# Memory-attention heads with a longer distance from scores to transposes, S5 phases by angle doubling, u tiles in the key buffers, and the last output tile in halves

## The chip, the cores and the metric

The kernel runs on one core of one Trainium2 chip. The metric is the device time of one execution in microseconds; a time quoted as "of the runs" is the median of several executions, and the profile is one further execution recorded by the hardware profiler. The engines are TensorE (PE, its weight loads PEld), VectorE (DVE), ScalarE (ACT), GpSimd (POOL) and SyncE (SP, which here only issues DMAs).

## What is computed

One layer of an encoder block, for a prompt of 256 tokens and a sample of 512 tokens together (768 rows, width 1024), all in 32-bit floats:

```python
h = rmsnorm(x, norm_mix_g)
u, q, k, v, qm, gl = split(h @ w_in)
# A) S5: bidirectional complex-diagonal scan over u (64 groups of 16 channels, 64 states each)
lam_bar = exp(lam * dt);  b_bar = ((lam_bar - 1) / lam) * b
s[t] = lam_bar * s[t-1] + b_bar @ u[t];   y = Re(c @ s)  (forward + backward) + d * u
z = gelu(y); s5_out = z * sigmoid(z @ s5_w_glu)
# B) differential attention, 8 heads, two softmax maps per head
# C) cross-attention of qm into 256 memory tokens, 4 heads of 256 channels:
kv = rmsnorm(mem) @ w_kv; q, k = rmsnorm per head
p = softmax(q @ k.T / 16); mem_out = p @ v
x = x + (sum over branches of sigmoid(gl + b_gate) * (branch @ w_branch)) @ w_out
x = x + (silu(h2 @ w_gate) * (h2 @ w_up)) @ w_down        # h2 = rmsnorm(x)
```

The outputs are the two blocks of rows of x.

## The kernel before

Every large product is done with each operand split into a high and a low part (suffixes `h` and `l`), as three matmuls of 128 x 128 weights against 256 or 512 columns (`mm3`, lines 831 to 833). `split_evac` (823, 824) makes the two parts of a PSUM result: ACT copies the high part, DVE subtracts. Weights arrive through `WStream`: SP loads a raw tile `wr` (567), ACT makes `wh` (666), DVE makes `wl` (672).

The program is written as one long Python function, `hybrid_block`. Dense projections are the base load of PE; the smaller stages are generators that are advanced between dense units by a `Pace` object: each dense unit calls `tick(w)`, and the generator makes `rate * w` steps. The written order is not the final one. A planner of the compiler takes the written order as priority, simulates the engines with its own costs, and fixes one order for each engine at compile time; on the chip each engine then works through its own queue strictly in that order, waiting on semaphores. A tile is given a buffer by name (`tag`) with a number of buffers (`bufs`); a new tile of a tag waits until the tile that held its buffer is done with, and a pool that takes over the memory of a closed pool waits for what lay there.

The stages around the change, with their places in the profiled execution:

- **Memory keys, values and queries** (from the start to about 212 us): `MEM_ORDER` k0 k1 v0 v1 k2 q0 q1 v2 k3 q2 v3 q3. The raw keys of a head lie in `kr` (three buffers in the pool `ma1`, right side of SBUF). `mem_q` writes the head's queries into `mqh`/`mql`, one buffer each, so the queries of head h+1 can be written only after the last scores of head h.
- **Memory attention**, `mem_attend`, paced through these units from q1 on and on through the first u chunks: for each head it sums squares (`qss`, 1008), makes the reciprocal root `rq`, and then takes the six tiles of 128 rows. Step i does the scores of tile i (`ms`, six matmuls into one of two PSUM banks of pool `a`; DVE takes the maximum, 1037; ACT the exponential, 1042; DVE normalizes `mp`, 1044), and the two transposes of tile i-1 (`mpT`, 1054). After two tiles ACT and DVE move the transposed weights into `pTh`/`pTl`, and in steps 3 and 7 PE multiplies them with the values (`mo`), which go to HBM (`mo_scr`, SP, 1027).
- **S5 parameters**, `S5.params` and `S5.pack`: short DVE instructions on 128 x 64 numbers, paced through the same units; ACT adds two sines of half the angle (`sn`, `cs`) and two of eight times the angle (`th8`, results `xr` and `p8r`, lines 138 and 140). `pack` scales matrices into `par` tiles (ACT copies, 263 and 264; DVE, 230) and stores them (`p_scr`).
- **u chunks**, `u_chunk` (from 215 us): the S5 input u is computed in four chunks of two tiles `ut`. POOL clears three columns of a new tile (293), DVE and ACT copy the PSUM results in (1183, 1181), and SP flushes the tile to HBM (`u_scr`, 298). Chunks 0 and 1 take their tiles from a pool `utp` of two buffers on the left side of SBUF; chunks 2 and 3 from `utp2` on the right side, where `ma1` was.
- **S5 steps**, `S5.steps` (from about 273 us): 16 groups, in 57 pieces, paced through u chunks 2 and 3 and the 12 gate chunks `gl`. `fetch` loads `par` on SP (280, 281) into the pool `s5q` on the left side; `build` makes `G` on DVE (308 to 317); `response` multiplies `G` (`psK`, 343).
- **Differential attention**, `diff_attend`, paced through the q/k/v units and, at `DIFF_TAIL` steps a unit, through the first branch product `br` (877 to 984 us); its scores are `sc` (1380, 1381), its transposes `aT`, its value products `av` (1417).
- **The last products**, `down_last`: two halves of the rows, each with two column blocks of three tiles of 128 x 512; `into` adds each PSUM bank to `x` (1626) and SP stores it (1628).

Of the kernel before, what the change touches and what calls it, by code (L numbers as in the profile page):

```python
# [24 lines left out]
class S5:  # L25
# [32 lines left out]
    def params(self, scratch):  # L58
# [85 lines left out]
        yield from exp_parts(ldt, dt)  # L144
        xr = tt(t("xr"), lre, dt, mul)
        th = tt(t("th"), lim, dt, mul)
        er, em1 = t("er"), t("em1")
        yield from exp_parts(xr, er, em1)
        thr = reduce_2pi(th, th)
        yield  # L150
        sn, cs = sincos(tsc(t(), thr, 0.5, None, mul), t("sn"), t("cs"))
        th8 = reduce_2pi(t("th8"), tsc(t(), thr, 8.0, None, mul))
        tsc(self.v8, th8, 1.0 / TWO_PI, None, mul)
        yield
        p8i, p8r = sincos(th8, xr, t("p8r"))
        s2 = tt(t(), sn, sn, mul)
        cm1 = tsc(t("cm1"), s2, -2.0, None, mul)
        sinth = stt(t(), sn, 2.0, cs, mul, mul)
        Lr = stt(t("Lr"), cm1, 1.0, er, add, mul)
        Li = tt(t("Li"), er, sinth, mul)  # L160
        yield

# [35 lines left out]
        pwi = scratch.tile([128, 8, 64], F32, name="pwi")  # L198
        tmp = scratch.tile([128, 4, 64], F32, name="pwt")
        nc.gpsimd.memset(pwr[:, 0, :], 1.0)  # L200
# [87 lines left out]

    def u_tile(self, pool, mt):

        ut = pool.tile([128, 8, NK], F32, name=f"ut{mt}", tag="ut")
        for c in (0, 33, 98):
            self.nc.gpsimd.memset(ut[:, :, c : c + 1], 0.0)
        return ut
# [212 lines left out]
TILES = 6  # L507
S5_RATE = 0.68
PAR_RATE = 0.7
PACK_RATE = 0.8  # L510
MEM_RATE = 1.45
DIFF_TAIL = 1.8
DIFF_RATE = 6.0 / 9.0
# [184 lines left out]
def hybrid_block(ctx, tc, A, outs, consts):  # L698
# [20 lines left out]
    def uid(s):  # L719
        cnt[0] += 1  # L720
        return f"{s}_{cnt[0]}"
# [275 lines left out]
    def mem_attend():  # L997

        for h in range(4):
# [13 lines left out]
            P, PT = {}, {}  # L1013
            for i in range(TILES + 2):
                if i in (3, 7):
                    sg = 0 if i == 3 else 1
                    c0, n = SEGS[sg]
                    for e in range(2):
                        mo = [k2.tile([128, 512], F32R, name=uid("mo" + w), tag="mo" + w) for w in "hl"]
                        ps = env.psb("mo")  # L1020
                        es = slice(128 * e, 128 * e + 128)
                        for c in range(2):
                            mm3(ps[:, 0:n], vv[0][:, 2 * sg + c, es], vv[1][:, 2 * sg + c, es],
                                PT[0][:, c, 0:n], PT[1][:, c, 0:n], c == 0, c == 1)
                        split_evac(mo[0][:, 0:n], mo[1][:, 0:n], ps[:, 0:n])
                        for w in range(2):
                            nc.sync.dma_start(mo_scr[w][:, 2 * h + e, c0 : c0 + n], mo[w][:, 0:n].bitcast(F32))
                if i < TILES:
# [10 lines left out]
                    v.tensor_tensor(out=nm, in0=nm, in1=r_, op=mul)  # L1039
                    p = k2.tile([128, 256], F32, name=uid("mp"), tag="mp", bufs=2)  # L1040
                    s = sm.tile([128, 1], F32, name=uid("mss"), tag="mss")
# [3 lines left out]
                    P[tt] = p  # L1045
                if 1 <= i <= TILES:
                    tt = i - 1
                    sg = 0 if tt < 2 else 1
# [4 lines left out]
                    for c in range(2):  # L1053
                        pe.transpose(pT[:, 256 * c + 128 * t : 256 * c + 128 * t + 128],
                                     p[:, 128 * c : 128 * c + 128], env.ident)
                    if tt in (0, 2):
                        PT = tuple(P3["k3"].tile([128, 2, 512], F32R, name=uid("pT" + w), tag="pT" + w) for w in "hl")
# [128 lines left out]

    mat.rate = 1.5
    def both(w):
# [8 lines left out]
    qctx.close()  # L1197
    uctx = ExitStack()
    up = uctx.enter_context(tc.tile_pool(name="utp2", bufs=2, side="right"))

    with ExitStack() as c2:
# [3 lines left out]
        pace = Pace(s5.steps(y_scr), S5_RATE)  # L1205
        u_chunk(2, pace.tick)
        u_chunk(3, pace.tick)
# [414 lines left out]

    def into(r, c, y, done=False):
        for t in range(3):
            o = out_block(r, c, t)
            v.tensor_tensor(out=o, in0=o, in1=y[t], op=add)
# [6 lines left out]
    def rows_times(ps, left_, right_, start, stop):  # L1633
# [46 lines left out]
    def down_last(fb):  # L1680
# [3 lines left out]
        for r in range(2):  # L1684
            h = slice(HT * r, HT * r + HT)
            x = [L.pop("A11") if r == 0 else left("A21", a[:, :, h]), left("A2", b[:, :, h])]
            if r == 0:
                down_sums(1)
                down_sums(2)
            ps = [banks(), banks()]  # L1690
            for i in range(2):
                for c in range(2):
                    y = [(lambda k, j=j: w[i](k, 512 * c, 512)[j]) for j in range(2)]
                    rows_times(ps[c], x[i], y, i == 0, i == 1)
            for c in range(2):
                into(r, c, ps[c], done=True)

# [453 lines left out]
```

## Time and profile before

| | |
|---|---|
| median of 3 runs | 1741.17 us (1739.56 to 1742.98) |
| the profiled execution | 1741.41 us |
| its span, first to last instruction | 1739.3 us |
| PE busy | 1713.9 us (99%), 11312 matmuls |
| DVE busy | 1340.6 us (77%) |
| ACT busy | 935.9 us (54%) |
| mean granted TensorE clock | 0.996 |

The execution's time is 2.1 us more than its span. A busy PE in these pages means that some matmul was in flight, not that it ran at its peak. A view of waits lists who sat idle until whom; a view of windows gives busy time and the granted clock (1.00 is full speed) in a stretch; the chain is the work that ended last, followed back.

### The profile page before, as it was taken

Reading aid. Unit: us, or ns where it says so; the run is one execution under the profiler, and the core shown is the slowest. Engines: PE = TensorE matmul, PEld = TensorE weight load, DVE = VectorE, ACT = ScalarE, POOL = GpSimd, SP = SyncE. Lnnn points to the kernel's source line nnn. Section 1 sums busy time; section 2 is a strip of 40 time slices with the busy share of each in tenths; the row PEclk is TensorE's granted clock in tenths of the full one; section 3 lists DMA queues with packets and bytes.
Section 4 is the critical chain, followed back from the end, with each engine's and each line's share of the span. In section 5 each row is a group of like instructions: output and inputs, shape, how many; then the busy total and the mean of one; then the engine's idle time right before and its main releaser. Section 6 shows DMA issues by size and latency. Waiting matters only on the chain.

```text
span 1739.3 us, 29776 instructions
## 1 busy us (share of the span) xinstructions
PE 1713.9 (99%) x11312; PEld 1581.8 (91%) x11312; DVE 1340.6 (77%) x2454; ACT 935.9 (54%) x1911; POOL 292.9 (17%) x306
## 2 busy tenths in 40 slices
PE   9989999999999999999999999999999999999998
PEld 9979887888888999999988898998889898989897
DVE  6876756899988458898877697793678878787876
ACT  6545634866566347877766564452434444444441
POOL 0000000000000011110211120440113334343430
PEclk9989999999999999999999999999999999999999
DMA  9413356675766536755793455663304547475643
GB/s 323 137 60 110 111 143 155 174 192 150 183 165 166 142 81 129 151 134 133 195 173 107 148 161 170 148 184 129 85 25 127 146 110 176 127 170 133 158 128 109
DMA packets 202478, 249.90 MB, mean 144 GB/s; under 512 B 33712, under 2 KB 155840, under 8 KB 202336
## 3 DMA queue, kind: packets, MB, share of 16 engines
q1 hardware_dynamic: 158800, 155.83, 29.4%
q0 software_dynamic: 32448, 67.01, 20.1%
q10 hardware_dynamic: 11088, 25.18, 4.2%
q8 instruction: 89, 1.46, 0.3%
q14 instruction: 53, 0.43, 0.1%
HBM read 173.51 MB, written 52.17 MB: 130 GB/s over the span
## 4 chain that ended last, share of the span: by engine, by line
PE 80%; issue 13%; DVE 3%; DMA 2%; ACT 2%; POOL 1%; SPq 0%; POOLq 0%; ACTq 0%; DVEq 0%
PE br L832 4%; PE br L833 4%; PE br L831 4%; PE up L831 3%; PE up L832 3%; PE up L833 3%; PE gate L832 3%; PE gate L833 3%; PE gate L831 3%; PE dn L831 3%; PE dn L833 3%; PE dn L832 3%; PE qk L833 3%; PE qk L831 3%; PE qk L832 3%
## 5 line engine op out<-in xcount | busy, mean ns | idle before, releaser
L666 ACT ACTIVATE wh<-wr 128x1024 fp32r<-128x1024 f32 x118 | 134.0, 1137 | 80.1 <-PE gl L832 19.2
L672 DVE TENSOR_TENSOR wl<-wr,wh 128x1024 fp32r<-128x1024 f32 x72 | 96.2, 1336 | 52.5 <-ACT wh L666 50.4
L831 PE MATMUL gl<-Hhi,wh 128*128 128x256 f32 (+1 forms) x384 | 133.1, 347 | 0.0
L833 PE MATMUL gl<-Hhi,wl 128*128 128x256 f32 (+1 forms) x384 | 129.3, 337 | 0.0
L832 PE MATMUL gl<-Hlo,wh 128*128 128x256 f32 (+1 forms) x384 | 129.3, 337 | 0.0
L670 POOL DMA_DIRECT2D wl<-wr x46 | 40.1, 879 | 465.4 <-ACT wl L669 457.6
L831 PE MATMUL qk<-wh,Hhi 128*128 128x256 f32 x384 | 108.0, 281 | 0.0
L832 PE MATMUL qk<-wl,Hhi 128*128 128x256 f32 x384 | 107.9, 281 | 0.0
L833 PE MATMUL qk<-wh,Hlo 128*128 128x256 f32 x384 | 107.7, 280 | 0.0
L591 DVE TENSOR_TENSOR wl_S<-ws,wh_S 128x512 fp32r<-128x512 f32 x91 | 69.3, 781 | 23.1 <-ACT wh_S L586 22.6
L586 ACT ACTIVATE wh_S<-ws 128x512 fp32r<-128x512 f32 x91 | 54.1, 625 | 60.8 <-PE up L832 27.2
L831 PEld LDWEIGHTS gl<-Hhi,wh 128*128 128x128 f32 x384 | 72.2, 188 | 10.2 <-issue 2.2
L833 PEld LDWEIGHTS gl<-Hhi,wl 128*128 128x128 f32 x384 | 72.2, 188 | 9.2 <-issue 0.6
L832 PEld LDWEIGHTS gl<-Hlo,wh 128*128 128x128 f32 x384 | 72.3, 188 | 7.6
L831 PEld LDWEIGHTS qk<-wh,Hhi 128*128 128x128 f32 x384 | 72.1, 188 | 0.9
L833 PEld LDWEIGHTS qk<-wh,Hlo 128*128 128x128 f32 x384 | 72.1, 188 | 0.5
L832 PEld LDWEIGHTS qk<-wl,Hhi 128*128 128x128 f32 x384 | 72.1, 188 | 0.5
L1386 DVE TENSOR_REDUCE nm<-sc 128x1 f32<-128x512 f32 (+1 forms) x96 | 56.7, 597 | 14.3 <-PE sc L1381 13.6
L1388 ACT ACTIVATE p<-sc,nm 128x512 f32<-128x512 f32 (+1 forms) x96 | 59.0, 617 | 11.0 <-DVE nm L1386 10.6
L612 POOL TENSOR_TENSOR ws<-wr,ws 128x512 f32<-128x512 f32 x26 | 40.0, 1539 | 119.5 <-DVE wl_S L591 119.5
L586 ACT ACTIVATE wh_A<-wr 128x512 fp32r<-128x512 f32 x65 | 38.0, 623 | 35.6 <-PE up L832 16.5
L1565 DVE TENSOR_TENSOR fs<-fs,up 128x384 f32<-128x384 f32 x70 | 37.5, 548 | 24.0 <-PE up L833 23.2
(695 smaller groups left out, 6229.9 us busy)
## 6 DMA issues: line engine op xcount, KB each, us to landing
wr<-in_w_in_dram SPq DMA_DIRECT2D x48, 512.0 KB, 4.5
wl<-wr POOLq DMA_DIRECT2D x46, 512.0 KB, 5.6
wr<-in_w_gate_up_dram SPq DMA_DIRECT2D x44, 512.0 KB, 4.2
wr<-in_w_branch_dram SPq DMA_DIRECT2D x24, 512.0 KB, 3.6
wr<-in_w_down_dram SPq DMA_DIRECT2D x22, 512.0 KB, 4.6
wr<-in_w_mem_kv_dram SPq DMA_DIRECT2D x16, 512.0 KB, 4.8
wr<-in_w_in_dram SPq DMA_DIRECT2D x32, 256.0 KB, 4.6
p_scr<-de ACTq DMA_DIRECT2D x27, 256.0 KB, 4.5
```

Of the source, the lines that this page charges most:

```text
L586: self.nc.scalar.activation(f(hi), src, AF.Copy)
L591: self.nc.vector.tensor_tensor(out=f(lo), in0=src, in1=f(hi).bitcast(F32), op=ALU.subtract)
L612: gt(out=s4, in0=A12, in1=s2, op=sub)
L666: self.nc.scalar.activation(hi, r, AF.Copy)
L670: self.nc.gpsimd.dma_start(lo, r.bitcast(F32R), accum_op=ALU.add)
L672: self.sub.tensor_tensor(out=lo, in0=r, in1=hi.bitcast(F32), op=ALU.subtract)
L831: pe.matmul(ps, wh, xh, start=start, stop=False)
L832: pe.matmul(ps, wh, xl, start=False, stop=False)
L833: pe.matmul(ps, wl, xh, start=False, stop=stop)
L1386: v.tensor_reduce(out=nm[:, m : m + 1], in_=ps, axis=AX.X, op=ALU.max, negate=True)
L1388: act.activation(pm[:, 0:n], ps, AF.Exp, bias=nm[:, m : m + 1], accum_out=s1s[:, tt : tt + 1] if m == 0 else s2)
L1565: v.tensor_tensor(out=o, in0=x, in1=y, op=add)
```

## The change

- `mem_attend` makes `TILES + 4` steps for a head where it made `TILES + 2`. The scores stay in steps 0 to 5; the transposes of tile i come in step i+2 where they came in i+1; the value products come in steps 5 and 9 where they came in 3 and 7. The tiles `mp` have three buffers, in another pool, where they had two. `MEM_RATE` goes from 1.45 to 1.6, and the rate in the u chunks from 1.5 to 1.75.
- `S5.params` no longer takes sine and cosine of eight times the angle from ACT. It doubles the angle three times on DVE from the sine and cosine that it has. `tmp` is made earlier and holds `xr`, `th`, `sn` and `cs`.
- The `ut` tiles of u chunks 0 and 1 take the `kr` buffers of the memory keys; the pool `utp` goes. A tile of 14,400 bytes a partition, never used, stands in front of `utp2`, so that `utp2` lies over the pool `ma2` and not over `ma1`.
- The first of the four paced units of u chunk 2 makes no S5 step; `S5_RATE` goes from 0.68 to 0.69.
- `DIFF_TAIL` goes from 1.8 to 2.0.
- The last tile of the last column block of the last rows is computed in two halves of 256 columns, in two PSUM banks, each added and stored by itself.

```diff
@@ S5.params
-        xr = tt(t("xr"), lre, dt, mul)
-        th = tt(t("th"), lim, dt, mul)
+        tmp = scratch.tile([128, 4, 64], F32, name="pwt")
+        xr = tt(tmp[:, 0], lre, dt, mul)
+        th = tt(tmp[:, 1], lim, dt, mul)
...
-        sn, cs = sincos(tsc(t(), thr, 0.5, None, mul), t("sn"), t("cs"))
+        sn, cs = sincos(tsc(t(), thr, 0.5, None, mul), tmp[:, 2], tmp[:, 3])
         th8 = reduce_2pi(t("th8"), tsc(t(), thr, 8.0, None, mul))
         tsc(self.v8, th8, 1.0 / TWO_PI, None, mul)
         yield
-        p8i, p8r = sincos(th8, xr, t("p8r"))
         s2 = tt(t(), sn, sn, mul)
         cm1 = tsc(t("cm1"), s2, -2.0, None, mul)
         sinth = stt(t(), sn, 2.0, cs, mul, mul)
         Lr = stt(t("Lr"), cm1, 1.0, er, add, mul)
         Li = tt(t("Li"), er, sinth, mul)
+        p8i, p8r = sinth, tsc(t(), cm1, 1.0, None, add)
+        yield
+        for i in range(3):
+            last = i == 2
+            s2 = tt(t(), p8i, p8i, mul)
+            p8i = stt(th if last else t(), p8i, 2.0, p8r, mul, mul)
+            p8r = tsc(xr if last else s2, s2, -2.0, 1.0, mul, add)
         yield
...
-        tmp = scratch.tile([128, 4, 64], F32, name="pwt")
@@ S5.u_tile
-    def u_tile(self, pool, mt):
+    def u_tile(self, pool, keys, mt):
 
-        ut = pool.tile([128, 8, NK], F32, name=f"ut{mt}", tag="ut")
+        if pool is None:
+            ut = keys.tile([128, 4, 256], F32, name=f"ut{mt}", tag="kr", bufs=3)
+            ut = ut.rearrange("p a b -> p (a b)")[:, 0 : 8 * NK].rearrange("p (j k) -> p j k", k=NK)
+        else:
+            ut = pool.tile([128, 8, NK], F32, name=f"ut{mt}", tag="ut")
@@ constants
-S5_RATE = 0.68
+S5_RATE = 0.69
-MEM_RATE = 1.45
-DIFF_TAIL = 1.8
+MEM_RATE = 1.6
+DIFF_TAIL = 2.0
@@ mem_attend
-            for i in range(TILES + 2):
-                if i in (3, 7):
-                    sg = 0 if i == 3 else 1
+            for i in range(TILES + 4):
+                if i in (5, 9):
+                    sg = 0 if i == 5 else 1
...
-                    p = k2.tile([128, 256], F32, name=uid("mp"), tag="mp", bufs=2)
+                    p = P3["k3"].tile([128, 256], F32, name=uid("mp"), tag="mp", bufs=3)
...
-                if 1 <= i <= TILES:
-                    tt = i - 1
+                if 2 <= i <= TILES + 1:
+                    tt = i - 2
...
-                    if tt in (0, 2):
+                    if tt in (1, 3):
                         PT = tuple(P3["k3"].tile([128, 2, 512], F32R, name=uid("pT" + w), tag="pT" + w) for w in "hl")
@@ hybrid_block, u chunks
-    up = uctx.enter_context(tc.tile_pool(name="utp", bufs=2))
+    up = None
...
-            ut = s5.u_tile(up, 2 * c + m)
+            ut = s5.u_tile(up, k1, 2 * c + m)
...
-    mat.rate = 1.5
+    mat.rate = 1.75
...
+    uctx.enter_context(tc.tile_pool(name="upad", bufs=1, side="right")).tile([128, 3600], F32, name="upad")
     up = uctx.enter_context(tc.tile_pool(name="utp2", bufs=2, side="right"))
...
-        u_chunk(2, pace.tick)
+        u_chunk(2, lambda w, n=iter(range(4)): pace.tick(w) if next(n) else None)
@@ into, rows_times, down_last
-            o = out_block(r, c, t)
-            v.tensor_tensor(out=o, in0=o, in1=y[t], op=add)
-            if done:
-                nc.sync.dma_start(os_[3 * r + t][:, 512 * c : 512 * c + 512], o)
+            for p, h in halves if halves and t == 2 else ((y[t], slice(0, 512)),):
+                o = out_block(r, c, t)[:, h]
+                v.tensor_tensor(out=o, in0=o, in1=p, op=add)
+                if done:
+                    nc.sync.dma_start(os_[3 * r + t][:, 512 * c + h.start : 512 * c + h.stop], o)
...
-            for k in range(2):
-                mm3(ps[t], lh[:, k, sl], ll[:, k, sl], rh(k), rl(k), start and k == 0, stop and k == 1)
+            for o, h in halves if halves and t == 2 else ((ps[t], slice(0, 512)),):
+                for k in range(2):
+                    mm3(o, lh[:, k, sl], ll[:, k, sl], rh(k)[:, h], rl(k)[:, h], start and k == 0, stop and k == 1)
...
+            halves = r and [(o[:, 0:256], slice(256 * j, 256 * j + 256)) for j, o in enumerate((ps[1][2], psd("dn")))]
```

More of the change, by code (lines that the diff above doesn't have):

```diff
@@ L1621, in out_block, with into, rows_times @@
         return x1[3 * r + t][:, 512 * c : 512 * c + 512]
[L1623 removed]
+    def into(r, c, y, done=False, halves=None):
         for t in range(3):
[L1625 to L1628 removed]
+            for p, h in halves if halves and t == 2 else ((y[t], slice(0, 512)),):
[3 more added lines that the diff above has]
+                    nc.sync.dma_start(os_[3 * r + t][:, 512 * c + h.start : 512 * c + h.stop], o)
     def banks():
         return [(psd if t else env.psb)("dn") for t in range(3)]
[L1633 removed]
+    def rows_times(ps, left_, right_, start, stop, halves=None):
         (lh, ll), (rh, rl) = left_, right_
@@ L1693, in down_last @@
                     y = [(lambda k, j=j: w[i](k, 512 * c, 512)[j]) for j in range(2)]
-                    rows_times(ps[c], x[i], y, i == 0, i == 1)
+                    rows_times(ps[c], x[i], y, i == 0, i == 1, c and halves)
             for c in range(2):
-                into(r, c, ps[c], done=True)
+                into(r, c, ps[c], done=True, halves=c and halves)
     def down_sums(t):
```

## The prediction

> **What bounds the kernel now.** I read the page's busy times first, then the view of PE's waits, because with PE this busy only its gaps and its clock are to be had.
>
> ```profile
> PE 1713.9 (99%) x11312; PEld 1581.8 (91%) x11312; DVE 1340.6 (77%) x2454; ACT 935.9 (54%) x1911; POOL 292.9 (17%) x306
> ```
>
> ```profile
> PE ms L831 <- ACT mp L1042: 4.1, 2, 2.1
> PE psK L343 <- issue: 2.5, 1, 2.5
> PE mpT L1054 <- DVE mp L1044: 2.4, 2, 1.9
> PE mo L831 <- ACT pTh L823: 2.2, 1, 2.2
> PE av L1417 <- ACT aT L1405: 2.2, 2, 1.4
> PE mq L831 <- ACT mqsq L985: 1.3, 1, 1.3
> PE sc L1380 <- ACT p L1388: 0.6, 1, 0.6
> ```
>
> The columns are total us, times, longest. PE is in flight for 1713.9 of 1739.3 us. The waits shown sum to 15.3 us, and all but the two of the attention's tail (`av`, `sc`, 2.8 us) lie in the memory attention and at the start of S5. The change adds no dense work and takes none away, so its worth is what becomes of these waits, of the end of the kernel, and of the clock. For the clock I asked for windows of 5 us; PE's busy time is the second number, the granted clock the one before the DMA share:
>
> ```profile
> 105.00:110.00 5.00, 3.49 (x16) 3.49 (x17) 3.56 (x19) 3.16 (x9) 0.00 (x0) 0.59 0.00 2
> 110.00:115.00 5.00, 3.66 (x11) 2.79 (x10) 5.00 (x22) 2.77 (x7) 0.00 (x0) 0.50 0.16 52
> 115.00:120.00 5.00, 5.00 (x22) 4.03 (x22) 3.33 (x10) 1.49 (x2) 0.00 (x0) 0.88 0.00 0
> 125.00:130.00 5.00, 5.00 (x45) 5.00 (x44) 0.69 (x1) 0.60 (x1) 0.00 (x0) 1.00 0.12 40
> 280.00:285.00 5.00, 2.35 (x39) 1.82 (x39) 5.00 (x7) 1.82 (x4) 0.18 (x3) 0.84 0.39 95
> 285.00:290.00 5.00, 5.00 (x29) 4.63 (x28) 5.00 (x11) 0.00 (x0) 0.00 (x0) 0.82 0.90 189
> ```
>
> Work that runs at clock c loses (1 - c) of its time. Behind the waits of the first memory head that is 3.49 x 0.41 + 3.66 x 0.50 + 5.00 x 0.12 = 3.9 us, behind the S5 start 2.35 x 0.16 + 5.00 x 0.18 = 1.3 us. A wait here thus costs about half as much again behind it.
>
> **The first memory head, 98 to 112 us.** The chain of work shows what PE waits for, and PE's timeline the four waits in brackets:
>
> ```profile
> 98.34 1.28 ACT L1042
> 99.64 1.20 ACT mp L1042 x4
> 100.86 1.28 ACT L140
> 102.15 0.35 ACT p8r L140
> 102.53 0.23 DVE fr L72
> 102.76 0.34 DVE mnm L1037
> ...
> 104.51 1.28 ACT L1042
> 105.80 0.66 ACT mp L1042 x2
> ```
>
> ```profile
> 100.34 0.38 PE L831 MATMUL ms<-kTh,mqh 128*128 128x256 f32 x1 [2.09 <-ACT mp L1042]
> 104.08 0.44 PE L1054 MATMUL mpT<-ident,mp 128*128 128x128 f32 x2 [1.87 <-DVE mp L1044]
> 106.51 0.58 PE L831 MATMUL ms<-kTh,mqh 128*128 128x256 f32 x1 [1.99 <-ACT mp L1042]
> 112.06 0.80 PE L831 MATMUL mq<-Hhi,wh 128*128 128x512 f32 x1 [1.34 <-ACT mqsq L985]
> ```
>
> ```profile
> L1037 DVE TENSOR_REDUCE mnm<-ms 128x1 f32<-128x256 f32 x4 | 1.7, 422 | 0.5 <-PE ms L833 0.5
> L72 DVE TENSOR_TENSOR s5t<-s5t,s5t 128x64 f32<-128x64 f32 x8 | 1.8, 222 | 0.2
> ```
>
> The pieces of 1.28 us without a tile are loads of ACT's function table. The first exponentials are followed by the cosine `p8r`, which needs the table of sines, and the next exponentials need theirs again. Worse, DVE's queue holds `fr`, which reads `p8r`, in front of the maximum `mnm` of the third score tile, so the softmax waits for the sine as well. Meanwhile dense work stands still: the queries of head 1 cannot leave PSUM before head 0's last scores.
>
> Without the sines of `th8` the loads at 100.86 and 104.51 go, 2 x 1.28 = 2.6 us, and nothing on DVE waits for ACT there. The third scores start at 100.34 and take about 0.7 us (six matmuls at 5.00 / 45 = 0.11 us), the maximum 0.42, its product about 0.2, so the third exponential can start near 101.8 and not at 105.80. The wait of 1.99 us then goes. The 1.87 us of `mpT` go too, since the transposes now stand one score tile later in PE's queue. The first wait stays (it ends with the first exponential, whose table load at 98.34 stays), and so does the last. That is -3.9 us of waits. With the rest the clock should hold, another -3.9: together **-7.7** (-3.8 to -11 as bounds: the clock stays halved, or all four waits go).
>
> [...]
>
> [...]
>
> Added there: ten short DVE instructions for the doublings against one that goes, 9 x 0.222 = 2.0 us of DVE at most. They lie beside the table load and the first exponentials unless the planner puts some in front of a maximum: **+0.6** (0 to 2.0).
>
> **The other memory waits.** Later `mo` waits 2.2 us for `pTh`, and `mpT` once more for 2.4 - 1.87 = 0.5 us. ACT's timeline shows why:
>
> ```profile
> 192.48 0.39 ACT L263 ACTIVATE par<-pwr 64x128 f32<-64x128 f32 x1
> ...
> 197.42 0.41 ACT L264 ACTIVATE par<-pwi 64x128 f32<-64x128 f32 x1
> 197.86 0.60 ACT L823 ACTIVATE pTh<-mpT 128x512 fp32r<-128x512 f32 x1
> ```
>
> Twelve `par` copies, 192.48 to 197.83, stand in front of `pTh`. With `mo` two steps behind its transposes, where it was one, PE has one step more of work before it: a unit is 24 matmuls of 256 columns, 24 x 0.11 = 2.7 us, so a step is 2.7 / 1.6 = 1.7 us of dense work and its own scores, about the 2.2 us. **-2.6** (0 to -2.7). The rates keep pace: ten pieces a head become twelve, 30 units x 1.45 = 43.5 become 48, 12 x 1.5 = 18 become 21. Two more pieces a head cost PE nothing, they hold no new matmuls.
>
> **The start of S5.** The chain, then SP's waits:
>
> ```profile
> 265.90 6.81 DMA u_scr<-ut
> 272.98 0.35 SPq L280
> 273.85 2.18 DMA par<-in_s_cd_dram
> ...
> 279.52 2.36 DVE G L308 x2
> ```
>
> ```profile
> SPq L280 <- DMA u_scr<-ut: 4.4, 1, 4.4
> 261.33 0.34 SPq L1027 DMA_DIRECT2D mo_scrl<-mol x1
> 267.61 0.42 DVE L1183 COPY ut<-u 128x256 f32<-128x256 f32 x1
> ```
>
> The first `fetch` waits at the head of SP's queue for the flush of the last `ut`, since `s5q` takes over `utp`'s memory; behind it queue the other fetches, the loads of U and the weights. The chain is in `G` until 279.52 + 2.36 = 281.9, 9 us after the fetch, and PE waits 2.5 us in front of `psK`. With the u tiles on the right side nothing on the left waits for that flush. What is late next is the memory attention's own memory on the left, done with before its last flush at 261.33, so the fetch can go some 10 us earlier, into a stretch where SP's next `wr` load is not yet due. Beginning the S5 steps one unit later adds a dense unit in front of `psK`. Both cover 2.5 us well: -2.5 and the clock's -1.3, **-3.8** (0 to -3.8). The moved `utp2` now waits for the last `mo` flush, issued at 261.33; its first copy is due at 267.61, over 6 us later, and the stores of the outputs land in 2.0 us (row below), so I cost it at nothing; without that cover it delays one PSUM copy. S5's own pieces come out even (84 units' weight are paced before, 83 after): 84 x 0.68 = 57.1 against 83 x 0.69 = 57.3, with 57 to make.
>
> **The end.**
>
> ```profile
> 1734.95 0.69 DVE L1626 TENSOR_TENSOR x<-x,dn 128x512 f32<-128x512 f32 x1 [0.67 <-PE dn L833]
> DMA to landing us min/median/max: 2.0/2.0/2.2
> ```
>
> After the last matmul come one addition of 512 columns and one store. Half of it is 0.42 us by the 256-column copy above: -0.27; the store of half the bytes is little shorter. **-0.3** (0 to -0.6).
>
> **The attention's tail.** At 2.0 steps a unit the written order of the differential attention runs ahead of `br` sooner, and its last steps should find dense work. 2.8 us of waits are there, but the steps are also bound by their own softmax chain through two PSUM banks. **-1.0** (-2.8 to +1).
>
> **What the planner does elsewhere.** Each of these edits draws the order of the whole program anew. A new wait like the old ones costs 0.5 to 2.5 us, and 1.3 more if the clock drops. **+1.5** (0 to +7).
>
> The sum is -7.7 + 0.6 - 2.6 - 3.8 - 0.3 - 1.0 + 1.5 = -13.3 us. Against the profiled execution (1739.3 of span and 2.1 around it, 1741.4, within 0.3 us of the median of the runs) that is 1728.1, said as **1728 us**.
>
> **The rivals.** First, the score chain of head 0 stays too slow: DVE's queue, now richer by the doublings, still holds the maxima up, PE's rest of waits still halves the clock. Then 3.9 us of clock come back and the 1.99 us wait with it: -13.3 + 5.9 = -7.4, 1734 us. For it speaks DVE, 3.56 and 5.00 of 5 us busy in the windows from 105; against it, that the late maximum stood behind `fr` and so behind a table load.
>
> Second, S5 gains nothing, because the planner puts `psK` earlier by as much as `G` gets earlier: -13.3 + 3.8 = -9.5, 1732 us. The skipped unit speaks against it.
>
> Third, the change does what it says and the planner's new order gives nearly all of it back, through new waits in the stretches from 300 us on: 1739 us, no difference. Against it: the waits removed have causes of their own in tables and buffers, whatever the order.
>
> Fourth, slower: the faster pace of the memory attention. Before, 2.7 / 1.45 = 1.84 us of dense work lay between two steps, now 1.67. Scores go through two PSUM banks, each held until its exponential is done; heads 1 to 3 show no such wait now (both `ms` waits, 4.1 us, are head 0's). If PE reaches the third scores of two later heads before the exponentials, each pays head 0's price, 7.3 us of waits and 3.9 of clock, 11.2 us: -13.3 + 22.4 = +9.1, 1750 us. It decides the sign from a little over one such head; the 9% less cover makes that unlikely.
>
> **How the numbers follow.** Forecast 0.55, with its own range 1722 to 1732 (all waits gone and the tail's too; or twice the planner's price and more); first rival 0.18; second 0.10; third 0.11; fourth 0.06. About 0.2% of the time, 3.5 us, is what a measurement of this kernel can tell from no change: below 1737.7 is faster. The forecast, the first two rivals and a fifth of the third give 0.86 faster; the rest of the third less its slow edge 0.07 the same; 0.07 slower. The range 1722 to 1737 leaves out some 0.05 below and 0.14 above.
>
> **What would show it.** Right: no table load of sines between the exponentials of head 0; clock 1.00 in all windows from 95 to 120 and from 275 to 295; no `psK`, `mpT` or `mo` wait over 1 us; the first `par` fetch near 262 us; a last addition of 256 columns. Wrong: two or more `ms` waits beyond head 0, a window below 1.00 at a new place, or PE waits from 300 us on that sum to more than 5 us.

## The result, and the profile after

The changed kernel takes 1737.51 us, the median of 12 runs (1735.18 to 1742.02), the kernel before 1741.09 us in 12 runs beside it. The ratio is 0.9978, with a 95% interval of 0.9968 to 0.9987: faster by about 3.6 us. The forecast was 1728 us, with a range that ended at 1737. So the sign was right, and the size was not: a little over a quarter of the 13.3 us came.

The profiled execution of the changed kernel took 1740.24 us (span 1738.3). Its lines of code carry numbers up to 11 higher than those of the kernel before (the scores L841 for L831, the `par` copies L269 and L270 for L263 and L264). First the engines' busy times on the page and the view of PE's waits (total us, times, longest), which answer to the two views with which the prediction began:

```profile
PE 1713.7 (99%) x11324; PEld 1581.2 (91%) x11324; DVE 1340.6 (77%) x2464; ACT 933.4 (54%) x1907; POOL 291.9 (17%) x306
```

```profile
PE ms L841 <- ACT mp L1052: 7.2, 4, 2.6
...
PE av L1428 <- ACT aT L1416: 2.2, 2, 1.4
PE br L842 <- DMA Hlo<-mo_scrl: 1.8, 1, 1.8
PE u L841 <- DVE ut L1193: 1.1, 1, 1.1
PE mpT L1064 <- DVE mp L1054: 1.1, 2, 0.7
PE psK L353 <- ACT Ysb L469: 0.9, 1, 0.9
PE sc L1391 <- ACT p L1399: 0.9, 1, 0.9
PE br L841 <- DMA Hhi<-mo_scrh: 0.9, 1, 0.9
```

Three of the old lines are gone (`mo` for `pTh`, `mq`, `psK` for the fetch). But `ms`, the scores, wait 7.2 us where they waited 4.1, there are waits of `u` and of `psK` at another place, and `br`, the product of the branches, waits 1.8 and 0.9 us for the loads of H where the kernel before had 0.6 and 0.2, which the prediction's list leaves out. The windows of 5 us, with the granted clock before the DMA share:

```profile
105.00:110.00 5.00, 2.82 (x17) 2.09 (x17) 5.00 (x28) 4.00 (x14) 0.00 (x0) 1.00 0.00 2
110.00:115.00 5.00, 5.00 (x15) 3.90 (x16) 4.51 (x18) 1.84 (x6) 0.00 (x0) 0.66 0.00 0
280.00:285.00 5.00, 5.00 (x59) 4.22 (x58) 4.93 (x9) 0.43 (x2) 0.00 (x0) 1.00 0.12 24
285.00:290.00 5.00, 5.00 (x31) 4.37 (x30) 1.79 (x5) 0.60 (x1) 0.00 (x0) 1.00 1.12 210
885.00:890.00 5.00, 5.00 (x19) 3.99 (x18) 3.01 (x6) 2.64 (x6) 0.53 (x1) 0.66 0.00 0
```

The start of S5 has its full clock, as forecast. The first memory head still has a stretch at half clock (0.66 in the window from 110), and a new one (0.66 from 885) stands behind the waits of `br`.

To say where the time went I cut each execution at the start of the same matmuls and take differences of those starts in the trace (us). "Memory" runs from the 145th matmul `mq`, shortly before head 0's softmax, to the first `u`: all waits of the memory heads lie in it.

| stage | before | before, again | after | after, again | e12 | e4 | e5 | e9 |
|---|---|---|---|---|---|---|---|---|
| start to 145th mq | 91.5 | 92.5 | 92.1 | 92.2 | 92.1 | 92.4 | 92.4 | 92.3 |
| memory, to first u | 123.5 | 121.4 | 120.8 | 120.8 | 115.8 | 115.8 | 120.4 | 113.1 |
| S5's start, first to last u | 87.5 | 87.0 | 84.3 | 83.9 | 86.8 | 83.9 | 83.1 | 83.6 |
| last u to last v | 574.8 | 574.8 | 575.7 | 575.6 | 574.8 | 575.6 | 575.7 | 575.6 |
| last v to last br | 295.1 | 295.1 | 298.9 | 295.6 | 300.7 | 300.2 | 300.5 | 294.7 |
| last br to the end | 566.9 | 566.8 | 566.5 | 566.6 | 566.9 | 566.8 | 566.8 | 567.9 |
| span | 1739.3 | 1737.6 | 1738.3 | 1734.6 | 1737.0 | 1734.6 | 1738.9 | 1727.3 |

"Again" are second profiles of the same kernels; the columns with numbers are experiments told below. Against the means of the two, memory gained 1.7 us where 9.7 were forecast, S5's start 3.1 of 3.8, the end 0.3 of 0.3; `last u to last v` lost 0.9, and from the last `v` to the last `br` the loss was 3.8 in one execution and 0.5 in the other.

**Why head 0 stays slow.** DVE's timeline of the changed kernel, lines of the reciprocal root `rq` (L1020 to L824) and of the softmax, with some of S5's parameters between them; then ACT's:

```profile
95.49 0.17 DVE L1020 TENSOR_SCALAR qs<-qss 128x6 f32<-128x6 f32 x1 [0.80 <-PE qss L1018]
95.57 0.22 DVE L83 SCALAR_TENSOR_TENSOR pwt<-s5t,pwt 128x64 f32<-128x64 f32 x1
...
100.01 0.16 DVE L824 SCALAR_TENSOR_TENSOR rqy<-rqt,rqy 128x6 f32<-128x6 f32 x1
...
100.56 0.22 DVE L1049 TENSOR_TENSOR mnm<-mnm,rqy 128x1 f32<-128x1 f32 x2
...
102.05 0.55 DVE L178 RECIPROCAL s5t<-s5t 128x64 f32<-128x64 f32 x1
...
103.05 0.42 DVE L1047 TENSOR_REDUCE mnm<-ms 128x1 f32<-128x256 f32 x1
```

```profile
98.71 1.28 ACT L1052 ACT_TABLE_LOAD   x1
100.75 0.56 ACT L1052 ACTIVATE mp<-ms,mnm,rqy 128x256 f32<-128x256 f32 x1 [0.76 <-DVE mnm L1049]
...
104.44 0.56 ACT L1052 ACTIVATE mp<-ms,mnm,rqy 128x256 f32<-128x256 f32 x1 [2.49 <-DVE mnm L1049]
```

Of the three table loads from 98 us on one is left, and ACT is done with it at 99.99; it then waits for DVE. The twelve small steps of the root take from 95.49 to 100.17, 4.7 us, because between any two of them stand one to six instructions of the parameters, 27 in all. In the kernel before the same steps took 3.0 us, 94.92 to 97.88, with 12 of them between:

```profile
94.92 0.16 DVE L1010 TENSOR_SCALAR qs<-qss 128x6 f32<-128x6 f32 x1 [0.81 <-PE qss L1008]
...
97.72 0.16 DVE L814 SCALAR_TENSOR_TENSOR rqy<-rqt,rqy 128x6 f32<-128x6 f32 x1
```

The first exponential starts at 100.75, 1.1 us later than before, and the third at 104.44 where it was 105.80. Head 0's waits are now five, 2.64, 0.36, 0.92, 0.70 and 1.27 us.

**Why the other memory wait stays.** ACT's timeline at head 2:

```profile
190.38 0.40 ACT L269 ACTIVATE par<-pwr 64x128 f32<-64x128 f32 x1
...
195.33 0.41 ACT L270 ACTIVATE par<-pwi 64x128 f32<-64x128 f32 x1
195.76 0.60 ACT L833 ACTIVATE pTh<-mpT 128x512 fp32r<-128x512 f32 x1
196.39 0.56 ACT L1052 ACTIVATE mp<-ms,mnm,rqy 128x256 f32<-128x256 f32 x1
```

The same twelve `par` copies stand in front of `pTh` and of the exponential behind it, as they did before. `mo` no longer meets them, the scores do: 2.40 us in front of `ms`, where it was 2.2 in front of `mo`.

### The profile page after: what moved, and what is told of

It is laid out like the page before. It is cut to its first block, busy times and chain, and to the rows that moved or that the text cites. A ratio compares the mean times of both kernels' runs of the same rounds, so it can differ in the third digit from the quotient of the medians.

```text
span 1738.3 us, 29797 instructions
## 1 busy us (share of the span) xinstructions
PE 1713.7 (99%) x11324; PEld 1581.2 (91%) x11324; DVE 1340.6 (77%) x2464; ACT 933.4 (54%) x1907; POOL 291.9 (17%) x306
## 4 chain that ended last, share of the span: by engine, by line
PE 80%; issue 13%; DVE 3%; DMA 2%; ACT 1%; POOL 1%; SPq 0%; POOLq 0%; DVEq 0%; ACTq 0%
PE br L842 4%; PE br L843 4%; PE br L841 4%; PE up L841 3%; PE up L842 3%; PE up L843 3%; PE gate L842 3%; PE gate L843 3%; PE gate L841 3%; PE dn L841 3%; PE dn L843 3%; PE dn L842 3%; PE qk L843 3%; PE qk L841 3%; PE qk L842 3%
## 5 line engine op out<-in xcount | busy, mean ns | idle before, releaser
L841 PE MATMUL gl<-Hhi,wh 128*128 128x256 f32 (+1 forms) x384 | 133.1, 347 | 0.0
L841 PE MATMUL qk<-wh,Hhi 128*128 128x256 f32 x384 | 108.1, 281 | 0.0
L841 PEld LDWEIGHTS gl<-Hhi,wh 128*128 128x128 f32 x384 | 72.2, 188 | 10.0 <-issue 2.2
L841 PEld LDWEIGHTS qk<-wh,Hhi 128*128 128x128 f32 x384 | 72.1, 188 | 0.9
```

The source lines that it names most:

```text
L841: pe.matmul(ps, wh, xh, start=start, stop=False)
```

## The experiments

Unless told otherwise each is the changed kernel with the one edit shown, and the time is the median, with the ratio to the kernel before on the same chip. My theory (Q in the expectations) was that the order of instructions in DVE's and ACT's queues makes the waits; the rival B, that the two PSUM banks for scores do.

**e1: the sines of `th8` on ACT again.**

```
- p8i, p8r = sinth, tsc(t(), cm1, 1.0, None, add)
- yield
- for i in range(3): ...
+ p8i, p8r = sincos(th8, xr, t("p8r"))
```

> The changed kernel, with sine and cosine of eight times the angle from ACT again instead of the doublings; all else as changed. Theory Q (what is left of PE's waits in the memory heads is set by what stands in front in the in-order queues of DVE and ACT): the two table loads and fr behind p8r come back, the doublings go from DVE; head 0's waits rise from 5.9 us (changed kernel) to about 7, the clock's loss with them; 2 to 4 us slower than the changed kernel, so about 1740. Rival B (the two PSUM banks of the scores set the pace of head 0, whatever is in the queues): within 1 us of the changed kernel's 1737.5.

1737.94 us, ratio 0.9977 (0.9965 to 0.9988): the same time as the changed kernel. Head 0's waits are 2.09, 1.74, 0.65, 0.35 and 0.78, together 5.6 us against 5.9. In the profile memory takes 122.7 us against 120.8, with two more stretches of 3.4 us at half clock in it, one at head 0 and one at 199 us. So the doublings and the two table loads that they replace are worth no more than the measurement can tell. Q had expected 2 to 4 us more and missed; by its time this run is as B expected. Its DVE shows what the doublings did: with the sines back (and the doublings gone) 12 parameter instructions stand between the root's steps again, and the root takes 3.0 us.

```profile
95.61 0.17 DVE L1014 TENSOR_SCALAR qs<-qss 128x6 f32<-128x6 f32 x1 [1.01 <-PE qss L1012]
...
98.41 0.16 DVE L818 SCALAR_TENSOR_TENSOR rqy<-rqt,rqy 128x6 f32<-128x6 f32 x1
```

The first exponential then waits for its table load and starts at 100.33, the third, behind the cosine and `fr` again, at 105.02. One delay stands in for the other.

**e2: one step from scores to transposes, with the old rates.**

```
- for i in range(TILES + 4):  if i in (5, 9): ...  if 2 <= i <= TILES + 1: tt = i - 2
+ for i in range(TILES + 2):  if i in (3, 7): ...  if 1 <= i <= TILES:     tt = i - 1
- MEM_RATE = 1.6, mat.rate = 1.75
+ MEM_RATE = 1.45, mat.rate = 1.5
```

> The changed kernel with one step from scores to transposes again (steps 0 to 7 of a head, rates 1.45 and 1.5); mp keeps its three buffers. The prediction's step: the longer distance is worth 1.9 us at head 0 and 2.6 us at the later heads, so 4 us slower than the changed kernel. Theory Q: the distance moves a wait from one instruction to another and takes little of it away: at head 2 the 2.4 us of ms become about 2.2 us of mo behind the same twelve par copies, at head 0 an mpT wait of 1 to 2 us comes back; 0 to 2 us slower, 1737.5 to 1739.5.

1738.72 us, ratio 0.998 (0.9969 to 0.9992), within the noise of the changed kernel. `mo` waits 2.2 us again in place of `ms`, as Q expected, and not the 4 us more of the prediction's step. Memory takes 121.8 us, 1.0 longer, but with two more stretches of 3.4 us at half clock at head 0 than the changed kernel has.

**e3: the u tiles in their own pool, no skipped unit.**

```
- up = None
+ up = uctx.enter_context(tc.tile_pool(name="utp", bufs=2))
- u_chunk(2, lambda w, n=iter(range(4)): pace.tick(w) if next(n) else None)
+ u_chunk(2, pace.tick)
```

(without the unused tile, too, and with `S5_RATE` 0.68 again)

> The changed kernel with the u tiles of chunks 0 and 1 in a pool of their own on the left again, no pad before utp2, no skipped unit, S5_RATE 0.68. If the first fetch was late because its memory waited for the last u flush: the fetch is issued near 270 us, psK waits 2 to 3 us, the clock falls for one window; the first gl matmuls come 3 us later than in the changed kernel; 1740 to 1741. Rival: the skipped unit or the planner's order made the gain, and the fetch stays early: within 1 us of 1737.5.

1738.78 us, ratio 0.9982 (0.9971 to 0.9992). In the trace the first `par` fetch is issued at 269.90 and not at 263.02, `psK` waits 2.4 us, 3.4 us at half clock follow, and S5's start takes 86.6 us against 84.3. In the trace this part of the change does what it says; the time lies under the 1740 to 1741 expected, and its interval overlaps that of the changed kernel. The wait of 0.94 us in front of a later `psK` is absent here: it came with this part too, and 0.8 of the 2.3 us are lost again by the last `v`.

**e4: S5's parameters held on DVE behind head 0's last maximum.** The units of head 1's queries pace no parameter step any more, and the steps paced later may be issued only after that maximum; their rate is raised from 0.7 to 0.93 so that they end in time.

```
+ i_ = v.tensor_tensor(out=nm, in0=nm, in1=r_, op=mul)
+ if (h, i) == (0, TILES - 1): env.held = i_
...
- par.tick(u_)
+ if (what, h) != ("q", 1):
+     with tc.issue_after(env.held.ins): par.tick(u_)
```

> The changed kernel, with the S5 parameters' DVE instructions held on DVE behind head 0's last maximum (same instructions, later; their pace raised from 0.7 to 0.93 to end at the same place). Theory Q: the reciprocal root then takes about 2.5 us and not 4.6, the first exponential starts near 98.5 us and not at 100.8, the maxima come at once; head 0's waits fall from 5.9 us to under 3, the clock stays 1.00 there; 3 to 5 us faster than the changed kernel, 1732.5 to 1734.5. Rival B (banks): the waits on the exponentials stay near 5 us and the time within 1 us of 1737.5.

1733.12 us, ratio 0.995 (0.993 to 0.997). DVE's and ACT's timeline, then the windows:

```profile
95.13 0.17 DVE L1020 TENSOR_SCALAR qs<-qss 128x6 f32<-128x6 f32 x1 [4.27 <-PE qss L1018]
...
97.35 0.17 DVE L824 SCALAR_TENSOR_TENSOR rqy<-rqt,rqy 128x6 f32<-128x6 f32 x1
97.55 0.23 DVE L1049 TENSOR_TENSOR mnm<-mnm,rqy 128x1 f32<-128x1 f32 x2
```

```profile
97.74 0.57 ACT L1054 ACTIVATE mp<-ms,mnm,rqy 128x256 f32<-128x256 f32 x1 [7.60 <-DVE mnm L1049]
...
100.56 0.56 ACT L1054 ACTIVATE mp<-ms,mnm,rqy 128x256 f32<-128x256 f32 x1 [1.61 <-DVE mnm L1049]
```

```profile
100.00:105.00 5.00, 3.35 (x25) 2.67 (x24) 4.69 (x17) 3.44 (x10) 0.00 (x0) 1.00 0.00 0
105.00:110.00 5.00, 4.75 (x29) 4.29 (x30) 4.89 (x20) 3.54 (x11) 0.00 (x0) 1.00 0.25 83
```

The root takes 2.4 us and not 4.7, the first exponential starts at 97.74, the third at 100.56. Head 0's waits are 0.28 and 1.54 us, the clock is never halved there, and memory takes 115.8 us. The time is as Q expected; the score banks are two as before, which speaks against B. But the hold clears ACT as well as DVE: the sines go with the parameters, and the table loads on either side of them, at 90.09 and 98.71 in the changed kernel, come at 125.56 and 136.43 here. Still there are the 2.4 us at head 2, and from the last `v` to the last `br`, where the loads of H are waited for, this execution takes 5 us more than the kernel before.

**e12: the same hold in the kernel before, and nothing else of the change.**

> The kernel before, with S5's parameters held on DVE behind head 0's last maximum and nothing else (the sines of th8 stay on ACT, the steps one apart, the u tiles in their pool). Theory Q: head 0's 7.3 us of waits and 3.9 us of half clock come from the parameters between the softmax's own instructions on DVE, and neither the doublings nor the two-step distance is needed for most of that: mv192 comes 4 to 7 us earlier than in the kernel before and the time falls 3 to 6 us, to 1735 to 1738 us. Rival T (the tables: without the doublings the sines' loads on ACT still delay exponentials somewhere): two or more extra table loads of 1.28 us now fall into head 1, waits of 2 us or more appear there, and the time falls by under 2 us.

1733.30 us, ratio 0.9952 (0.9934 to 0.9971), 9.6 us under the kernel before and more than Q expected. The waits from 80 to 300 us:

```profile
PE mo L831 <- ACT pTh L823: 2.4, 1, 2.4
PE psK L343 <- issue: 1.9, 1, 1.9
PE mo L831 <- DVE kTl L824: 1.3, 1, 1.3
PE ms L831 <- ACT mp L1044: 0.5, 1, 0.5
PE mpT L1056 <- DVE mp L1046: 0.5, 1, 0.5
```

Head 0 keeps 0.5 and 1.3 us with the sines on ACT and the steps one apart; memory takes 115.8 us, as in e4. Here, too, the sines leave head 0: the table loads around them, four in the kernel before (89.52, 98.34, 100.86 and 104.51), are two, at 126.68 and 135.96. So with the parameters out of the way, on DVE and on ACT, neither the doublings nor the two-step distance gains anything in the memory stage of these executions. How much of the gain is DVE's and how much ACT's, this run does not separate.

**e5: the `par` copies on GpSimd.**

```
- nc.scalar.activation(dst[0:64], lay(src[0:64]), AF.Copy)
+ nc.gpsimd.tensor_copy(dst[0:64], lay(src[0:64]))
```

(and the second half likewise)

> The two copies that lay out the S5 parameters (the twelve par copies) run on GpSimd and no longer on ScalarE. Theory Q (the order in an engine's queue makes the waits): the wait of 2.40 us in front of ms at 194.70 in the changed kernel ends with an exponential that stands behind pTh and the twelve copies on ACT; with the copies gone from ACT's queue, that wait falls under 0.5 us, the chain from the last mq to the first u is some 2 us shorter, and the time is about 2 us under the changed kernel's. Rival (the softmax chain through two PSUM banks is too slow for a step each unit, whatever stands on ACT): a wait of 2 us or more stays in front of ms or mo between 190 and 200 us, and the time is that of the changed kernel. Cost that could hide it: twelve copies on GpSimd take longer than 0.39 to 0.41 us each; if the transposes that read par then wait, the loss shows at the start of S5 and not here.

1736.75 us, ratio 0.997 (0.9959 to 0.9982). The waits from 180 to 300 us are these two:

```profile
PE ms L841 <- ACT mp L1052: 0.6, 1, 0.6
PE mpT L1064 <- DVE mp L1054: 0.5, 1, 0.5
```

The 2.40 us became 0.64 and 0.53, and the wait of `u` for DVE (1.13) is gone. Q's bound of 0.5 was a little missed. In the median only 0.8 us of it shows against the changed kernel, where Q expected about 2, with overlapping intervals; in this execution memory takes 120.4 us, with one more stretch at half clock at head 0 (mean granted clock of the execution 0.996, of the changed kernel's 0.998). In e9 memory takes 2.7 us less than in e4.

**e6: three PSUM banks for scores.**

```
- psum(0, d=3, a=2, b=3)
+ psum(0, d=2, a=3, b=3)
```

> Three PSUM banks for the score tiles of the memory heads where there were two; one bank fewer for the dense groups. Theory Q: the scores of head 0 wait for exponentials that are late because of what stands on DVE in front of the maxima; a third bank lets PE go on by one score tile, but the transposes behind need the same late exponentials, so that the waits of head 0 (5.9 us in the changed kernel) move from ms to mpT or mo and keep at least 4 us of their sum; time within 2 us of the changed kernel, or slower for the missing bank. Rival B (two banks are the bound): the waits of head 0 and the 2.40 us at 194.70 fall to under 2 us together, the windows from 98 to 120 and 190 to 200 show clock 1.00, and the time is 5 us or more under the changed kernel's.

1747.77 us, ratio 1.0032 (1.0017 to 1.0047): slower. The waits from 80 to 300 us:

```profile
PE ms L841 <- ACT mp L1052: 9.1, 2, 7.5
PE ms L841 <- ACT kTh L833: 2.2, 1, 2.2
PE psK L353 <- issue: 2.2, 1, 2.2
```

With the third bank head 0 meets one wait of 7.5 us: its root is still at work on DVE at 103.7, between the same parameters. That speaks against B. But the missing bank of the dense groups changed the order everywhere, so the loss, 6 us against the kernel before and 10 against the changed one, is not the bank's price alone.

**e7: the last loads of H issued by SyncE.**

```
- gp.dma_start(H[w][:, :, t], mo_scr[w][:, :, t])
+ if n_v == 5: nc.sync.dma_start(H[w][:, :, t].bitcast(F32), mo_scr[w][:, :, t])
+ else: gp.dma_start(H[w][:, :, t], mo_scr[w][:, :, t])
```

> The last pair of loads of H from the scratch of the memory output, in front of the product of the branches, is issued by SyncE's queue and not by GpSimd's. In the changed kernel's execution these loads took 10.9 us from issue to the last packet, PE came to them 7.4 us after the issue, and waited 0.88 and 1.81 us with 3.4 us at half clock behind (about 4.4 us in all); in the kernel before 8.7 us and 0.24 and 0.57 us. Theory D (the transfer's length is GpSimd's queue's): by SyncE's queue they land within 8 us, both waits fall under 0.3 us, no half-clock window near 885, time about 2 to 4 us under the changed kernel's. Rival (512-byte packets on 16 engines, whoever issues them, or what else is in the queues at that time): 8.7 to 11.3 us again, the same two waits of 0.2 to 2.2 us, and the time within 1 us of the changed kernel's; if SyncE issues them behind other loads of its queue, later still.

**e10 and e11: the changed kernel and the kernel before, each profiled once more.**

> The changed kernel once more, for a second profile. If the length of the last loads of H (10.9 us from issue to the last packet, waits of 0.88 and 1.81 us, half clock behind) belongs to the kernel, it comes again within 0.5 us. If it changes from execution to execution, as the nine profiles at hand with the same order of issues suggest (8.7 to 12.0 us), it comes anywhere from 8.7 to 12 us, and the execution is 2 to 4 us shorter where it is short.

> The kernel before once more, for a second profile: the same question. In its first profile the loads took 8.7 us and PE waited 0.24 and 0.57 us without a half-clock window behind. Belongs to the kernel: 8.7 us again within 0.5. Changes from execution to execution: anywhere from 8.7 to 12 us. The waits of head 0 (7.3 us) and of psK (2.5 us) come again within 0.3 us in either case.

e7: 1735.28 us, ratio 0.9968 (0.9954 to 0.9981). Its waits from 860 to 900 us, and those of the changed kernel profiled again:

```profile
PE br L842 <- DMA Hlo<-mo_scrl: 0.7, 1, 0.7
```

```profile
PE br L842 <- DMA Hlo<-mo_scrl: 1.2, 1, 1.2
PE br L841 <- DMA Hhi<-mo_scrh: 0.3, 1, 0.3
```

The same kernel waited 0.9 and 1.8 us here in its first profile, with 3.4 us at half clock behind, and 0.3 and 1.2 in its second, with none; its loads took 10.9 and then 8.9 us from issue to the last packet. The two executions took 1740.24 and 1736.62 us. So this loss is not shown to be the change's: the loads take 8.5 to 12.1 us over the twelve profiles with GpSimd, with the same issues at the same distance, and e12, the kernel before with the hold alone, waited 3.8 us for them. Issued by SyncE, one wait of 0.7 remained (0.9 in e9), more than the 0.3 expected. Against the second profile, this trace has 0.8 us less of waits, against the first 2.0 us and the half clock, with the issues moved by at most 0.5 us against `br`. From issue to the last packet the loads took 8.9 us, and 9.0 in e9, not under 8 as expected; half of the twelve profiles with GpSimd are under 9.0 as well. So that SyncE makes the transfer shorter is not shown, and the interval of the time overlaps that of the changed kernel.

e11 has the waits of head 0 again (2.08, 1.86, 1.99 and 1.34; `psK` waits 2.0 us where it waited 2.5) but a different clock behind them:

```profile
105.00:110.00 5.00, 3.01 (x15) 2.77 (x16) 3.87 (x23) 2.98 (x7) 0.00 (x0) 0.79 0.00 2
110.00:115.00 5.00, 3.66 (x17) 2.96 (x17) 4.85 (x19) 3.45 (x9) 0.00 (x0) 0.87 0.08 26
```

0.79 and 0.87 where the first profile of the same kernel had 0.59, 0.50 and 0.88: one stretch of 3.41 us at half clock and not three in a row. With it goes the difference of 2.1 us between the memory stages of these two profiles of one kernel.

**e8: the attention's tail at 1.8 steps a unit and the last tile whole.**

```
- DIFF_TAIL = 2.0
+ DIFF_TAIL = 1.8
- halves = r and [...]
+ halves = None and [...]
```

> The pace of the differential attention's steps is 1.8 a unit again, and the last output tile is added and stored in one piece of 512 columns. The rest is the changed kernel. If the forecast's two terms hold (1.0 us for the tail, 0.3 us for the halves): 1.3 us slower than the changed kernel, waits of the tail (av, sc) 1 us less in the changed kernel than here. If, as the changed kernel's trace suggests, the pace gave nothing (tail waits 0.94, 1.38 and 0.85 us against 0.65, 1.38 and 0.85 before) and the halves 0.6 us less the 0.24 us that the last matmuls got longer: 0 to 0.4 us slower, tail waits 0.65, 1.38, 0.85 again, and a last addition of 0.67 us.

1738.15 us, ratio 0.998 (0.9971 to 0.999): not to be told from the changed kernel. Waits of the tail 0.72, 1.38 and 0.85 us, against 0.94, 1.38 and 0.85 in the changed kernel's first profile and 0.38, 1.38 and 0.85 in its second: the pace gave nothing. Last `br` to the end 566.85, against 566.48 and 566.62: the halves give 0.2 to 0.4 us by these two (the other profiles with halves, e9 aside, range from 566.2 to 566.8).

**e9: e4, e5 and e7 in one kernel.**

> The three edits that gained by themselves, in one kernel: S5's parameters held on DVE behind head 0's last maximum, the par copies on GpSimd, the last loads of H issued by SyncE. By the medians of the single runs against their runs of the kernel before (ratios .9950, .9970 and .9968, the changed kernel .9978) the sum over the changed kernel is -0.28 - 0.08 - 0.10 = -0.46%, so a ratio near .9932, about 1730 us. Theory Q (each wait has its own instruction ahead in a queue): the gains add, 1728 to 1732 us; waits in the first 300 us under 3 us in all, clock 1.00 from 95 to 300. Rival (what is saved early is paid again later, at the loads of H or at psK): within 1.5 us of the best single one, 1733.1 us.

1728.10 us (1727.33 to 1729.08), ratio 0.991 (0.9893 to 0.9926): 14.8 us faster than the kernel before beside it, and faster than the changed kernel. The waits from the start to 320 us:

```profile
PE warm L761 <- POOL ident masks.py:199: 2.7, 1, 2.7
PE mo L841 <- DVE kTl L834: 1.5, 1, 1.5
PE ms L841 <- ACT mp L1054: 0.9, 2, 0.6
PE u L841 <- DVE ut L1197: 0.6, 1, 0.6
PE mpT L1066 <- DVE mp L1056: 0.5, 1, 0.5
```

Apart from the warm-up 3.6 us are left, a little over the 3 expected, and the granted clock stays 1.00 from the warm-up to the end. The spread of the runs, 7 us over twelve in the changed kernel, is under 2 over four. One wait is new, 1.54 us of `dn` for `lA12l` at 1351 us, and costs the last stage 1.0.

## Why the prediction was wrong, point by point

- **What bounds the kernel: right.** The waits and the clock behind them were there to get, and e9 got most of them. That it landed on the forecast's own time is a coincidence: it got them by other means than the change.
- **The first memory head, -7.7 and +0.6: the step that failed.** It said that without the sines "nothing on DVE waits for ACT there", and so "the third exponential can start near 101.8". The first half is true, and ACT did lose two table loads. The second does not follow: the exponentials need the root and the maxima, and these stand in DVE's queue between S5's parameters, whether or not those wait for a sine. The sine had held the parameters back; with it gone they came at once, 27 between the steps of the root where there had been 12 (12 again in e1). The root took 4.7 us and not 3.0, ACT waited 0.76 us for its end, and the third scores, from whose start at 100.34 the prediction reckons, came at 101.46. Their maximum, taken at 103.05, was scaled at 104.25, and the third exponential came at 104.44. Waits fell from 7.3 to 5.9 us, by 1.4 and not 3.9. e4 (third exponential at 100.56) and e12 (the same 115.8 us without the rest of the change) show that the parameters are the cause. Both runs take them off DVE and ACT together. That it was DVE in the changed kernel is read from the timeline above, where ACT waits 0.76 and 2.49 us for `mnm` before the first and the third exponential.
- **The clock, -3.9: mis-sized, because it was read from one execution.** By the windows the kernel before lost 3.9 us of clock at head 0 in one execution and 3.01 x 0.21 + 3.66 x 0.13 = 1.1 in the other, the changed kernel 5.00 x 0.34 = 1.7 in both. The ratio that I used, half as much again behind the waits, is the first execution's (3.9 us behind 7.3 of waits); the second had 1.1 behind the same 7.3. The stretches at 0.50 at head 0 were 3.41 us long in the changed kernel and in e11 and 10.24 in the first profile of the kernel before, and came to 6.8 in e1 (0.67 and 0.65 in the windows from 105 to 115); no wait there is over 2.64 us in any of these profiles, and the clock fell behind them. What makes the same waits give one stretch or three no run here shows.
- **The doublings, +0.6:** no cost by themselves that e1 could tell. They are ten of the 47 parameter instructions on DVE between the start of the root and the third exponential, and five of the 27 between the root's steps.
- **The other memory waits, -2.6: failed, at "PE has one step more of work before it".** `mo` did get its step more. But the cause that the prediction itself quoted, twelve copies in a row on ACT, stayed, and the scores of the next step go through the same queue. The wait went from `mo` to `ms` at its full size (2.2 to 2.40); the 0.5 of `mpT` went. Only taking the copies off ACT (e5, e9) removed it.
- **The start of S5, -3.8: right in mechanism, near in size.** First fetch at 263.02 (forecast near 262), no `psK` wait (0.27 us in the second profile), clock 1.00: -3.1 in the trace. What took its place was not looked for: `u` waits 1.13 us (0.48 in the second profile) for a copy behind G and E on DVE, and 0.9 us are lost at a `psK` at 480 us.
- **The end, -0.3: right** (-0.3, by two profiles of each). **The attention's tail, -1.0: nothing**; its own softmax chain is the bound, as the prediction feared.
- **The planner elsewhere, +1.5:** 0.9 at `psK`. The stretch with the loads of H, at the start of `br`, adds 0.5 to 3.8 by execution; that this is the planner's is not shown.

With the measured terms, -1.7 for memory, -3.1, -0.3, 0, +0.9 and +0.5, the sum is -3.7, and the difference of the medians is -3.6. That is luck in part: the 0.5 is the second execution's, and with 2.1, the mean of the two, and 0.1 lost before the 145th `mq` the sum is -2.0, which is the difference of the mean spans. Of the rivals the first came nearest in mechanism: it named DVE's queue and the maxima. But it let that queue cost only 5.9 us of the 13.3 and put the blame on the doublings; and no rival joined it to the second memory wait. By the number the third, 1739, is nearer, and losses from 300 us on did come, but most of the largest one lies at the loads of H. The fourth, slower by the faster pace, did not come: heads 1 and 3 show no new waits of `ms`.

Not settled: what makes the last loads of H take 8.5 us in one execution and 12.1 in another, the exact price of a PSUM bank in e6, and the shares of DVE and ACT in what the hold gains.

## What to carry to other kernels

When a wait goes through an instruction that is itself delayed in an engine's queue (in DVE's timeline of the kernel before, the maximum at 102.67 stood behind `fr`, which had waited 0.65 us for `p8r`), ask what the queue will hold once the delay is gone: here the delayed work came forward and took the place of its own delay. Hold off-path work behind the last instruction of the critical chain by an explicit order, and then see whether the rewriting is still needed; in the memory stage here it was not. And read a stage from two executions before pricing the clock in it, for one draw can be as large as the effect: the two executions of the kernel before lost 3.9 and 1.1 us of clock at head 0, and the change gained 3.6 us in all.

## What the runs showed of the hardware that was not expected

The granted clock stood at 0.50 in pieces of 3.41 us. By an estimate, 3.41 x 0.50, each costs up to 1.7 us of dense work: in the piece at head 0 of the changed kernel the matmuls of 512 columns started 0.43 us apart from 111.24 on, and 0.23 to 0.24 apart from 114.33 on. Behind the same four waits of 1.3 to 2.1 us the kernel before had one piece (e11) or three (its first profile). Twelve copies of 64x128 took 0.40 to 0.45 us each on ACT and 0.40 to 0.55 on GpSimd, but two of those on GpSimd took 2.30 and 2.25 us and one 1.01 (2.31, 2.23 and 1.02 in e9, the same three of the twelve). The two long ones lie beside the two `wl` of DVE there (2.44 us from 189.11 and 2.13 from 192.20 in e5); that these are the cause no run here shows, and PE did not wait for the copies.
